# Three moves in the odd layer: where the last projection's first loads land, when attention outputs are transposed, and when the conditioning begins

## The chip, the cores and the metric

The kernel runs on one core of a Trainium2 chip. The metric is device time in microseconds: the median of three runs, 2327.63 us (2325.06 to 2328.44). A separate profiled execution took 2321.26 us, with a span of 2319.5 us between its first and last instruction; all rows of the trace are from that one.

## The reference

One step of a two-layer transformer trunk, for 128 prompt tokens and 512 sample tokens that share weights. Each layer normalizes, applies a shift and a scale that come from a conditioning vector (`silu(cond) @ ada_w + ada_b`, split in shift, scale and gate), projects, runs its mixers, multiplies by SiLU gates, projects out and adds the result times the conditioning gate:

```
hs = rms_norm(xs, norm_g[layer]) * (1.0 + sc_s) + sh_s
cq, ck, cv, cg, dq, dk, dv, dg = split_cols(h @ w_in, ODD_SPLIT)
o1 = attend(cq[:, 0], ck_all[:, 0], cv_all);  o2 = attend(cq[:, 1], ck_all[:, 1], cv_all)
o_c = rms_norm(o1 - lam * o2, c_on) * (1.0 - lam_init)
y_d = merge_heads(attend(q_d, dk_all, dv_all)) * silu(dg)
xs = xs + gt_s * (concat([o_c * silu(cg), y_d]) @ w_out)
```

The second (odd) layer has mixer D, eight heads of grouped-query attention, and mixer C, four heads of differential attention: two softmax maps whose difference weighs the values. The sample tokens attend to 256 cached keys and their own 512.

## The kernel before

All activations lie with features on the partitions and 640 tokens (512 + 128) in the free dimension. A float32 matrix product is made of three matmuls of split operands (`wh*hi`, `wh*lo`, `wl*hi`): ScalarE rounds the high part, VectorE subtracts the low part (`split`, line 241 and 242). A projection's weight column block of 128 is used in four quarters of four row tiles each; a quarter is 24 matmuls of 320 columns, half into `pa`, half into `pb` (lines 276 to 278).

The odd layer's queries and keys are projected by `run_tiles`: 30 jobs of four quarters, 120 quarters in all. After each quarter `slot` advances three kinds of side work: the preparation of the tile that has just been projected (`q_gen`, `k_gen`, `v_gen`), one step (for later jobs 1.1 or 1.5 on average) of a running attention generator, and `rate` steps of `fill1`. `fill1` is `ada_on_dve`: four blocks of the layer's conditioning product that VectorE makes by itself, as 64 multiply-adds into `acc` per block (lines 211 and 213) from weights `adaw` loaded by SyncE (line 207). A block can't begin before the instruction to which it is tied, the weight split that was the latest when the block was emitted (line 202). The tile framework then sets every engine's own order, and pulls instructions that are ready ahead of their place in the program.

`k_gen` transposes the projected keys, scales and rotates them on VectorE (from line 600 to 620, with a power on GpSimd, line 608, between), and TensorE transposes the result back (line 564). `diff_gen` runs one head of mixer C over five query blocks u: `score` (scores into the single PSUM tile `S`, softmax, the difference of the maps, line 1354), `groups` (transposes of the weights, line 732), `weigh` (18 matmuls with the values, lines 1369 to 1371, then the output's norm on VectorE, ScalarE and GpSimd, lines 1373 to 1380) and `out` (two transposes of the normalized `on`, line 1386, and the product with the gate, line 1391). A `yield` ends a step.

The last projection begins with `y1_maker`: for each of 16 row tiles k it loads `yin` from DRAM and splits it into the tile `h` that the matmuls read. The order of the row tiles is 0 to 3, 8 to 11, 12 to 15, 4 to 7. Tiles with k % 8 < 4 land in the buffers `rp` (three) and `stg` (two) (line 1536), which `very_late_gate` also uses for the last two jobs (lines 1486 to 1492); the others, after the pool of the odd layer is closed, in `xr` (line 1122). SyncE's DMA issues go in order: what stands behind a waiting one waits too.

Of the kernel before, what the change touches and what calls it, by code (L numbers as in the profile page):

```python
# [45 lines left out]
SPLIT_AHEAD = 3  # L46
N_FILL0 = 12
FILL0 = 1.2
FILL1 = 1.25
FILL1_FROM = 0  # L50


@with_exitstack
def trunk_kernel(ctx: ExitStack, tc: tile.TileContext, I: dict, O: dict):
# [12 lines left out]
    def psT():  # L67
        return pT.tile([P, 512], F32, tag="T", name="T")
# [226 lines left out]
    def drain(queue):  # L295
        while queue:
            advance(queue, 1)
# [440 lines left out]
    def scores(q, blk, k, segs, masks=()):  # L738
        s = pS.tile([P, 1024], F32, tag="S", name="S")
        bs = slice(blk * P, (blk + 1) * P)  # L740
        for dst, k0, n in segs:
            ms = [(m, o) for m, o in masks if dst <= o < dst + n]
            d, ks = s[:, dst:dst + n], slice(k0, k0 + n)
            PE.matmul(d, q[0][:, bs], k[0][:, ks], start=True, stop=False)  # L744
            PE.matmul(d, q[0][:, bs], k[1][:, ks], start=False, stop=False)
            PE.matmul(d, q[1][:, bs], k[0][:, ks], start=False, stop=not ms)  # L746
            for i, (m, o) in enumerate(ms):
                PE.matmul(s[:, o:o + P], identb, m, start=False, stop=(i == len(ms) - 1))
        return s
# [5 lines left out]
    def blk_plan(blk, banded):  # L755

        if blk == 4:
            return PROMPT_SEGS, (), P, 2 * P, [6]
        if not banded:
            return DENSE_SEGS, (), 128, 896, [0, 1, 2, 3, 4, 5]  # L760
        lo_b, hi_b = max(0, blk - 1), min(3, blk + 1)
        nb = (hi_b - lo_b + 1) * P
        masks = []
        if blk > 0:
            masks.append((mask_lo, 512))
        if blk < 3:
            masks.append((mask_hi, 512 + (blk + 1 - lo_b) * P))
        return ([(256, 0, CTX), (512, CTX + lo_b * P, nb)], masks, 256, 512 + nb,
                [0, 1] + [2 + b for b in range(lo_b, hi_b + 1)])
# [184 lines left out]
    def y_pair(i):  # L954
        t = pools["cur"].tile([P, 2, NT], F32, tag="y", name="y", bufs=3 - st["sets"])
        y[i], y[i + 1] = t[:, 0, :], t[:, 1, :]
        return t
# [376 lines left out]
    def diff_gen(ap, h, v, kq):  # L1334

        gt = gates_back(2 * h)
        t = y_pair(2 * h) if gt is None else gt
        ps, pts, ons, rls = {}, {}, {}, {}

        maps = []  # L1340

        def score(u, m):
            segs, masks, lo, hi, _ = blk_plan(u, False)
            n = hi - lo
            k, q = kq[m]
            s = scores(q, u, k, segs)
            maps.append(soft(ap, 768, s[:, lo:hi], n, q[2][u]))
            if m == 0:
                return
            pp, rr, ll = zip(*maps)  # L1350
            maps.clear()
            w = small.tile([P, 1], F32, tag="w", name="w")
            V.scalar_tensor_tensor(out=w, in0=ll[0], scalar=nlam, in1=rr[1], op0=ALU.mult, op1=ALU.mult)
            V.scalar_tensor_tensor(out=pp[0][:, 0:n], in0=pp[1][:, 0:n], scalar=w, in1=pp[0][:, 0:n],
                                   op0=ALU.mult, op1=ALU.add)
            ps[u], rls[u] = pp[0], rr[0]

        def groups(u):
            n = len(blk_plan(u, False)[4])
            pts[u] = [pt_group(ap, [ps[u][:, i * P:(i + 1) * P] for i in range(c0, min(c0 + 4, n))])  # L1360
                      for c0 in range(0, n, 4)]

        def weigh(u):
            chunks = blk_plan(u, False)[4]
            last = len(chunks) - 1
            o = psT()[:, 0:256]
            for i, c in enumerate(chunks):
                ph, pl = (x[:, (i % 4) * P:(i % 4) * P + P] for x in pts[u][i // 4])
                PE.matmul(o, ph, v[0][:, c, :], start=(i == 0), stop=False)
                PE.matmul(o, ph, v[1][:, c, :], start=False, stop=False)  # L1370
                PE.matmul(o, pl, v[0][:, c, :], start=False, stop=(i == last))
            on = ap.tile([P, 256], F32, tag="on", name="on", bufs=2)
            V.tensor_scalar(on, o, rls[u], None, ALU.mult)
            ssq = small.tile([P, 1], F32, tag="ssq", name="ssq")
            junk = ap.tile([P, 256], F32, tag="junk", name="junk")
            A.activation(junk, on, AF.Square, accum_out=ssq)
            V.tensor_scalar(ssq, ssq, 1.0 / 256, EPS, ALU.mult, ALU.add)
            rn = small.tile([P, 1], F32, tag="rn", name="rn")
            G.tensor_tensor(rn, ssq, half[:, 0:1], op=ALU.pow)
            V.scalar_tensor_tensor(out=on, in0=on, scalar=rn, in1=st["con"], op0=ALU.mult, op1=ALU.mult)  # L1380
            ons[u] = on

        def out(u):
            x = psT()
            for j in range(2):
                PE.transpose(x[:, j * P:(j + 1) * P], ons[u][:, j * P:(j + 1) * P], ident)
            d, x = t[:, :, u * P:(u + 1) * P], x[:, 0:256].rearrange("p (j q) -> p j q", j=2)
            if gt is None:
                A.copy(d, x)
            else:  # L1390
                V.tensor_mul(d, x, d)

        for u in range(7):
            if u >= 2:
                out(u - 2)
            if u < 5:
                score(u, 0)
            if 1 <= u < 6:
                groups(u - 1)
            if u < 6:  # L1400
                yield
            if u < 5:
                score(u, 1)
            if 1 <= u < 6:
                weigh(u - 1)
            if u < 6:
                yield
        save_y(2 * h, 2 * h + 1)
# [64 lines left out]
    def gates_back(i):  # L1473
        if i not in FRONT:
            return None
        t = y_pair(i)
        for j in range(2):
            nc.sync.dma_start(t[:, j, :], gdram[i + j])
        return t
# [36 lines left out]
    for i in (4, 5):  # L1516
        jobs.append((OD["cg"] + i * P, very_late_gate(i)))
    run_tiles(jobs, I["od_w_in"][0], None, fill1, FILL1, fill_from=FILL1_FROM,
              steps=lambda i: brisk.get(i, 1.0))
# [3 lines left out]
    def y1_maker(k):  # L1523
        if k == 12:
            for _ in fill1:
                pass
            drain(attn)
            close("odd")
            open_pool("fin")
            attn.append(forms(ydram))  # L1530
        if k % 8 >= 4:
            late_yin(k)
        else:
            tag, n = (("rp", 3), ("stg", 2))[k % 2]
            t = pools["cur"].tile([P, NT], F32, tag=tag, name="yin", bufs=n)
            nc.sync.dma_start(t, ydram[k])
            split(*new_h(k), t)
# [82 lines left out]
```

## Time and profile before

| | |
|---|---|
| median of three runs | 2327.63 us |
| the profiled execution | 2321.26 us, its span 2319.5 us |
| TensorE busy | 2259.1 us, 97% of the span |
| VectorE busy | 1678.2 us, 72% |
| ScalarE busy | 991.9 us, 43% |
| DMA | 348.18 MB, mean 150 GB/s |
| odd layer's `run_tiles` | begins near 1417 us; the last projection begins near 2075 us |

A busy TensorE is the state to keep, so the rows to read are those in which it stood idle: a row of the timeline gives start, duration, engine, line, operation and, in brackets, the idle time before it and the instruction that ended the idle time. In a row of waits stand the total, the number and the longest. The windows give busy time by engine with the number of instructions, and then the TensorE clock that was granted, as a share of full speed.

### The profile page before, as it was taken

To read this page: it belongs to the slowest core of one execution; us is meant where nothing else is said; L and a number is where in the kernel's file an instruction comes from. 1 tells how busy PE (TensorE), PEld (TensorE's weight loads), DVE (VectorE), ACT (ScalarE), POOL (GpSimd) and SP (SyncE) were. 2 spreads that over 40 slices of the span, in tenths; PEclk is the share of its full clock that TensorE was granted. 3 is DMA by queue.
4 is the path that set the end of the run, shared out by engine and by line. 5 is a ranking of instruction groups with operands and counts; after the bars stand their busy time and mean duration, and the time that the engine had idled before them with its cause. 6 is when DMAs were issued, how large, how long until landed. Compare 5 with 4: busy or idle time off the path is not lost.

```text
span 2319.5 us, 41525 instructions
## 1 busy us (share of the span) xinstructions
PE 2259.1 (97%) x15796; PEld 2182.4 (94%) x15796; DVE 1678.2 (72%) x3364; ACT 991.9 (43%) x2043; POOL 184.0 (8%) x251
## 2 busy tenths in 40 slices
PE   7999999999999999999999999999999999997999
PEld 5699999999999999999999999999999989997999
DVE  4559886786866664988877766778687696576576
ACT  4335432433422222544744445454555454553343
POOL 2110000000000000000100000000001111100001
PEclk9999999999999999999999999999999999999999
DMA  9974545445455543844763335333243333237532
GB/s 354 339 264 124 159 123 159 143 127 163 124 180 155 152 138 120 280 133 138 247 212 113 106 115 168 97 101 97 63 128 106 103 103 92 80 111 244 152 119 70
DMA packets 390056, 348.18 MB, mean 150 GB/s; under 512 B 19362, under 2 KB 327088, under 8 KB 389344
## 3 DMA queue, kind: packets, MB, share of 16 engines
q1 hardware_dynamic: 376960, 296.97, 41.8%
q0 software_dynamic: 12176, 46.39, 5.2%
q8 instruction: 124, 2.03, 0.4%
q10 hardware_dynamic: 720, 2.16, 0.2%
q14 instruction: 76, 0.62, 0.1%
HBM read 304.55 MB, written 40.90 MB: 149 GB/s over the span
## 4 chain that ended last, share of the span: by engine, by line
PE 84%; DVE 6%; DMA 4%; ACT 2%; issue 2%; POOL 1%; SPq 0%; POOLq 0%; ACTq 0%; DVEq 0%
PE pa L276 8%; PE pb L277 8%; PE pa L277 8%; PE pb L276 8%; PE pa L278 8%; PE pb L278 8%; PE pq L535 7%; PE pq L536 7%; PE pq L537 7%; PE T L732 2%; DMA adaw<-in_ada_w 2%; DMA yin<-yd 1%; PE T L178 1%; PE S L744 1%; PE S L746 1%
## 5 line engine op out<-in xcount | busy, mean ns | idle before, releaser
L241 ACT ACTIVATE wh<-raw 128x512 fp32r<-128x512 f32 (+1 forms) x442 | 273.4, 619 | 671.6 <-PE pb L277 565.5
L276 PE MATMUL pa<-h,wh 128*128 128x320 f32 x1520 | 483.8, 319 | 15.8 <-ACT h L241 13.3
L277 PE MATMUL pa<-h,wh 128*128 128x320 f32 x1520 | 474.0, 312 | 1.0 <-DVE h L242 0.6
L278 PE MATMUL pa<-h,wl 128*128 128x320 f32 x1520 | 472.4, 311 | 0.0
L278 PE MATMUL pb<-h,wl 128*128 128x320 f32 x1520 | 471.5, 310 | 0.0
L277 PE MATMUL pb<-h,wh 128*128 128x320 f32 x1520 | 471.0, 310 | 0.0
L276 PE MATMUL pb<-h,wh 128*128 128x320 f32 x1520 | 470.8, 310 | 0.0
L242 DVE TENSOR_TENSOR wl<-raw,wh 128x512 fp32r<-128x512 f32 (+1 forms) x442 | 297.2, 673 | 238.6 <-ACT wh L241 211.9
L213 DVE SCALAR_TENSOR_TENSOR acc<-adaw,sT,acc 128x512 f32<-128x512 f32 (+1 forms) x600 | 359.4, 637 | 12.4 <-DMA adaw<-in_ada_w 11.9
L276 PEld LDWEIGHTS pa<-h,wh 128*128 128x128 f32 x1520 | 286.8, 189 | 29.3 <-ACT h L241 14.9
L277 PEld LDWEIGHTS pa<-h,wh 128*128 128x128 f32 x1520 | 286.9, 189 | 6.0 <-DVE h L242 2.9
L278 PEld LDWEIGHTS pa<-h,wl 128*128 128x128 f32 x1520 | 286.6, 189 | 2.9 <-issue 2.9
L278 PEld LDWEIGHTS pb<-h,wl 128*128 128x128 f32 x1520 | 285.9, 188 | 2.1 <-issue 2.1
L276 PEld LDWEIGHTS pb<-h,wh 128*128 128x128 f32 x1520 | 286.0, 188 | 0.4 <-issue 0.4
L277 PEld LDWEIGHTS pb<-h,wh 128*128 128x128 f32 x1520 | 285.9, 188 | 0.1
L535 PE MATMUL pq<-h,wh 128*128 128x320 f32 x608 | 189.7, 312 | 0.7 <-ACT wh L241 0.7
L536 PE MATMUL pq<-h,wh 128*128 128x320 f32 x608 | 187.9, 309 | 0.0
L537 PE MATMUL pq<-h,wl 128*128 128x320 f32 x608 | 187.8, 309 | 0.0
L718 ACT ACTIVATE p<-S,nm,rq 128x768 f32<-128x768 f32 (+3 forms) x120 | 101.1, 843 | 100.7 <-DVE nm L713 59.5
L535 PE MATMUL pq<-T,wh 128*128 128x320 f32 x456 | 140.9, 309 | 0.0
L537 PE MATMUL pq<-T,wl 128*128 128x320 f32 x456 | 140.9, 309 | 0.0
L536 PE MATMUL pq<-T,wh 128*128 128x320 f32 x456 | 140.9, 309 | 0.0
(337 smaller groups left out, 3890.4 us busy)
## 6 DMA issues: line engine op xcount, KB each, us to landing
adaw<-in_ada_w SPq DMA_DIRECT2D x192, 256.0 KB, 2.9
raw<-in_ev_w_in SPq DMA_DIRECT2D x184, 256.0 KB, 2.9
raw<-in_od_w_in SPq DMA_DIRECT2D x160, 256.0 KB, 2.9
ada<-in_ada_w SPq DMA_DIRECT2D x14, 2048.0 KB, 10.3
adaw<-in_ada_w SPq DMA_DIRECT2D x128, 128.0 KB, 2.1
w<-in_od_w_in SPq DMA_DIRECT2D x24, 512.0 KB, 3.7
yd<-y POOLq DMA_DIRECT2D x32, 320.0 KB, 3.4
yin<-yd SPq DMA_DIRECT2D x32, 320.0 KB, 4.5
```

The lines of the kernel that those rows point to most:

```text
L178: PE.matmul(acc[32 * g:32 * g + 32, 0:wd], sT[:, kt, :], w[:, kt % m, :], start=(i < 4), stop=(i >= KT - 4), tile_position=(0, 32 * g))
L213: V.scalar_tensor_tensor(out=a, in0=w, scalar=sT[:, kt, c:c + 1], in1=a, op0=ALU.mult, op1=ALU.add)
L241: A.activation(hi, x, AF.Copy)
L242: V.tensor_sub(lo, x, hi)
L276: PE.matmul(ps, wh[:, i, :], hi[:, sl], start=(j == js[0] if alone else (pos == 0 and j == 0)), stop=False)
L277: PE.matmul(ps, wh[:, i, :], lo[:, sl], start=False, stop=False)
L278: PE.matmul(ps, wl[:, i, :], hi[:, sl], start=False, stop=(j == js[1] - 1 if alone else (pos == 3 and j == 3)))
L535: PE.matmul(ps, wh[:, j, :], hi, start=(h == 0 and j == 0), stop=False)
L536: PE.matmul(ps, wh[:, j, :], lo, start=False, stop=False)
L537: PE.matmul(ps, wl[:, j, :], hi, start=False, stop=(h == 1 and j == 3))
L718: A.activation(p[:, 0:n], s, AF.Exp, scale=rsc, bias=nm, accum_out=l)
L732: PE.transpose(t[:, i * P:(i + 1) * P], p, ident)
```

## The change

Three edits. `fill1` gets its first step after quarter 8 instead of at once, at 1.3 steps a quarter instead of 1.25. In `diff_gen` the call `out(u - 2)` moves behind the first `yield` of block u, so that it comes one step later, except for the last block's. In `y1_maker` the loads for k = 0 to 3 use the buffers `q0h`, `q0l`, `q1h`, `q1l`, which hold two sets of split queries in turn; the set that comes next is that of the head before the last.

```diff
-FILL1 = 1.25
-FILL1_FROM = 0
+FILL1 = 1.3
+FILL1_FROM = 8
...
         for u in range(7):
-            if u >= 2:
-                out(u - 2)
             if u < 5:
                 score(u, 0)
             if 1 <= u < 6:
                 groups(u - 1)
             if u < 6:
                 yield
+            if u >= 2:
+                out(u - 2)
             if u < 5:
                 score(u, 1)
...
-            tag, n = (("rp", 3), ("stg", 2))[k % 2]
+
+            tag, n = (("q0h", 2), ("q0l", 2), ("q1h", 2), ("q1l", 2))[k] if k < 4 else (("rp", 3), ("stg", 2))[k % 2]
             t = pools["cur"].tile([P, NT], F32, tag=tag, name="yin", bufs=n)
```

VectorE at the start of the odd layer, before. `lp` and `nlam` are the constants of mixer C, `acc` the conditioning sums, `wl` a weight split, `qm` the first query tile's rotation:

```order
L1319 TENSOR_REDUCE ls<-lp 128x2
L211 TENSOR_SCALAR acc_16206<-adaw,sT 128x256
L211 TENSOR_SCALAR acc_16207<-adaw,sT 128x256
L1322 TENSOR_TENSOR nlam<-le 128x1
L213 SCALAR_TENSOR_TENSOR acc_16206<-adaw,sT,acc_16206 128x256
```

The same place now, and the place at which the conditioning now begins, at the second query tile's `qm`:

```order
L1319 TENSOR_REDUCE ls<-lp 128x2
L1322 TENSOR_TENSOR nlam<-le 128x1
L1323 TENSOR_SCALAR nlam<-nlam 128x1
L242 TENSOR_TENSOR wl<-raw,wh 128x512
L242 TENSOR_TENSOR vl<-ctxv,vh 128x256
L242 TENSOR_TENSOR wl<-raw,wh 128x512
L656 TENSOR_TENSOR qm<-qx,tables 128x512
...
L656 TENSOR_TENSOR qm<-qx,tables 128x512
L202 CAST acc_16505<-wl 128x1
L202 CAST acc_16506<-wl 128x1
L211 TENSOR_SCALAR acc_16505<-adaw,sT 128x256
```

Sixty-one conditioning products stood ahead of the first key preparation (line 600) before; now 31 do, and the rest of the block stands behind it.

VectorE at the second key preparation of head 2 of mixer C (`kg` is its first row), before:

```order
L242 TENSOR_TENSOR k0l<-T,k0h 128x256
L242 TENSOR_TENSOR k0l<-T,k0h 128x512
L242 TENSOR_TENSOR k0l<-T,k0h 128x128
L242 TENSOR_TENSOR vl<-vx,vh 128x5x128
L242 TENSOR_TENSOR wl<-raw,wh 128x512 x2
L600 TENSOR_TENSOR kg<-T,gain_rows 128x512
```

The same place now:

```order
L213 SCALAR_TENSOR_TENSOR acc_21895<-adaw,sT,acc_21895 128x256
L213 SCALAR_TENSOR_TENSOR acc_21894<-adaw,sT,acc_21894 128x256
L242 TENSOR_TENSOR wl<-raw,wh 128x512
L213 SCALAR_TENSOR_TENSOR acc_21895<-adaw,sT,acc_21895 128x256
L213 SCALAR_TENSOR_TENSOR acc_21894<-adaw,sT,acc_21894 128x256
L213 SCALAR_TENSOR_TENSOR acc_21895<-adaw,sT,acc_21895 128x256
L213 SCALAR_TENSOR_TENSOR acc_21894<-adaw,sT,acc_21894 128x256
L213 SCALAR_TENSOR_TENSOR acc_21895<-adaw,sT,acc_21895 128x256
L242 TENSOR_TENSOR wl<-raw,wh 128x512
L213 SCALAR_TENSOR_TENSOR acc_21894<-adaw,sT,acc_21894 128x256
L213 SCALAR_TENSOR_TENSOR acc_21895<-adaw,sT,acc_21895 128x256
L213 SCALAR_TENSOR_TENSOR acc_21894<-adaw,sT,acc_21894 128x256
```

The conditioning's last block now lies over both key preparations of head 2 (ahead of the other one eight of its products stand within twelve rows); before, it lay over the second one of head 1.

TensorE at the fourth `out` of head 1 of mixer C, before. `on` is the normalized output, `p` the softmax weights, `h_12900` and the like the activations of a quarter; the block's last `weigh` stands 14 projection matmuls ahead of the `on` row:

```order
L276 MATMUL pa<-h_12900,wh 128x320
L277 MATMUL pa<-h_12900,wh 128x320
L278 MATMUL pa<-h_12900,wl 128x320
L276 MATMUL pb<-h_12882,wh 128x320
L277 MATMUL pb<-h_12882,wh 128x320
L1386 MATMUL T<-ident,on 128x128 x2
L732 MATMUL T<-ident,p 128x128
```

The same `out` now:

```order
L276 MATMUL pb<-h_13150,wh 128x320
L277 MATMUL pb<-h_13150,wh 128x320
L278 MATMUL pb<-h_13150,wl 128x320
L1386 MATMUL T<-ident,on 128x128 x2
L276 MATMUL pb<-h_13159,wh 128x320
L1369 MATMUL T<-vh,pth 128x256
```

It stands behind 39 projection matmuls after the same `weigh`, in the next quarter, and right ahead of the last block's `weigh`.

On SyncE the loads of row tiles 0 to 3 now stand among the weight loads of the last jobs, 13 weight loads earlier than before, and those of tiles 8 to 11 take the places that tiles 0 to 3 had. The loads of row tiles 12 to 15 (line 1122) and everything behind them stand as before.

## The prediction

> **What bounds the kernel now.** I read the page first, for the engine that is nearly always busy, then the windows over the part that the change touches, then TensorE's waits there, and the timeline at the longest of them.
>
> ```profile
> span 2319.5 us, 41525 instructions
> PE 2259.1 (97%) x15796; PEld 2182.4 (94%) x15796; DVE 1678.2 (72%) x3364; ACT 991.9 (43%) x2043; POOL 184.0 (8%) x251
> ...
> 1416.00:1780.00 364.00, 358.55 (x2528) 347.97 (x2527) 275.98 (x630) 184.83 (x397) 30.59 (x30) 1.00 0.37 113
> 1780.00:2097.00 317.00, 303.49 (x2115) 289.96 (x2113) 224.21 (x517) 159.19 (x388) 40.01 (x46) 1.00 0.31 94
> 2097.00:2127.00 30.00, 17.76 (x102) 16.38 (x103) 19.87 (x34) 11.03 (x16) 1.12 (x2) 0.89 0.82 271
> ```
>
> TensorE (first busy figure of a row) is the bound: work taken from another engine is worth nothing unless TensorE waited for it. In the two windows of the odd layer's projections and attentions it stood idle for 364.00 - 358.55 = 5.5 us and 317.00 - 303.49 = 13.5 us, and at the change to the last projection for 12.2 us of 30. That is all that the change can win, beside clock. TensorE's own waits over these windows, with total, number and longest:
>
> ```profile
> PE pa L276 <- ACT h L241: 12.6, 4, 8.4
> PE T L1386 <- DVE on L1380: 7.4, 8, 1.5
> PE T L564 <- DVE m L620: 3.8, 4, 2.1
> PE T L794 <- DVE ptl L242: 1.7, 2, 0.8
> PE S L744 <- ACT p L718: 1.6, 2, 1.1
> ...
> PE T L1386 <- DVE rl L724: 0.5, 1, 0.5
> PE T L564 <- DVE k1l L242: 0.4, 1, 0.4
> ```
>
> Three of these groups answer to the three edits: `h` split from loaded rows to the loads, `on` to the output transposes, `m` (the rotated keys) to the conditioning, which shares VectorE with the key preparation.
>
> ```profile
> 1472.69 0.66 PE L564 MATMUL T<-ident,m 128*128 128x128 f32 x4 [2.08 <-DVE m L620]
> ...
> 1608.68 0.38 PE L794 MATMUL T<-ptl,vh 128*128 128x256 f32 x1 [0.84 <-DVE ptl L242]
> ...
> 1841.82 0.44 PE L1386 MATMUL T<-ident,on 128*128 128x128 f32 x2 [1.45 <-DVE on L1380]
> 1860.92 0.66 PE L564 MATMUL T<-ident,m 128*128 128x128 f32 x4 [1.43 <-DVE m L620]
> 1863.05 0.33 PE L564 MATMUL T<-ident,kg 128*128 128x128 f32 x1 [0.42 <-DVE k1l L242]
> ...
> 1922.23 0.41 PE L1386 MATMUL T<-ident,on 128*128 128x128 f32 x2 [1.23 <-DVE on L1380]
> ...
> 1933.43 0.44 PE L1386 MATMUL T<-ident,on 128*128 128x128 f32 x2 [1.46 <-DVE on L1380]
> 2020.68 0.44 PE L1386 MATMUL T<-ident,on 128*128 128x128 f32 x2 [1.45 <-DVE on L1380]
> 2080.88 0.42 PE L276 MATMUL pa<-h,wh 128*128 128x320 f32 x1 [1.42 <-ACT h L241]
> 2105.17 0.64 PE L276 MATMUL pa<-h,wh 128*128 128x320 f32 x1 [8.37 <-ACT h L241]
> ```
>
> **Part 1: the conditioning eight quarters later.** The same 256 multiply-adds are made; nothing is added or taken away. They come in four bursts, one for each block, 66 instructions and some 27 us each, between which VectorE makes none:
>
> ```profile
> 1420.00:1480.00 60.00, 27.00 (x66) 0.97 0.58 176
> 1480.00:1540.00 60.00, 0.00 (x0) 1.00 0.18 53
> 1540.00:1610.00 70.00, 27.44 (x66) 1.00 0.40 120
> ...
> 1840.00:1920.00 80.00, 27.89 (x66) 1.00 0.43 130
> ```
>
> The first burst holds up the first key preparation:
>
> ```profile
> 1465.11 0.20 ACT L598 ACTIVATION_READ_ACCUMULATOR junk<-T 128x1 f32 x1
> ...
> 1465.34 1.28 DVE L213 SCALAR_TENSOR_TENSOR acc<-adaw,sT,acc 128x256 f32<-128x256 f32 x3 [0.16 <-DMA adaw<-in_ada_w]
> 1466.54 0.68 DVE L600 TENSOR_TENSOR kg<-T,gain_rows 128x512 f32<-128x512 f32 x1
> ...
> 1471.95 0.68 DVE L620 TENSOR_TENSOR m<-m,m 128x512 f32<-128x512 f32 x1
> ```
>
> ScalarE had squared the last transposed block by 1465.3, so VectorE could have scaled the keys before that; it came to them at 1466.54, behind conditioning that waited for its own weights. TensorE, which had nothing else in order, stood for 2.08 us. The price is more than that, because the clock (the third figure from the end of each row) went down behind it:
>
> ```profile
> 1470.00:1474.00 4.00, 1.92 (x15) 1.68 (x14) 3.97 (x9) 1.50 (x3) 0.60 (x1) 1.00 0.20 65
> 1474.00:1477.00 3.00, 3.00 (x14) 2.96 (x13) 0.98 (x2) 0.70 (x2) 0.00 (x0) 0.50 0.55 159
> 1477.00:1480.00 3.00, 3.00 (x21) 3.00 (x21) 0.69 (x1) 0.95 (x2) 0.00 (x0) 0.93 0.00 0
> ...
> 1933.00:1938.00 5.00, 4.57 (x33) 4.50 (x34) 4.66 (x9) 2.11 (x5) 1.11 (x2) 1.00 0.72 237
> ```
>
> Three microseconds at 0.50 lose 1.5, three at 0.93 lose 0.2: 1.7 us, so this wait costs 3.8. (The last row holds the gap of 1.46 us at 1933.43, which left the clock alone.) In the new order 31 of the conditioning's products stand ahead of that key preparation instead of 61. VectorE needs some 0.4 us for each (27.00 / 66), so 30 fewer take 12 us out of its way, while the start comes later by eight quarters; a quarter is 24 matmuls at the pace of these two rows, 0.15 us apart, so 3.6 us, and eight are 29 us:
>
> ```profile
> 1922.73 0.31 PE L276 MATMUL pb<-h,wh 128*128 128x320 f32 x1
> 1922.88 0.31 PE L277 MATMUL pb<-h,wh 128*128 128x320 f32 x1
> ```
>
> From a start near 1446 (the second query's rotation, with no backlog ahead of it), 31 products (12.7 us) and the queries' and weights' own instructions (some 4.6 us) bring VectorE to the keys at 1463 to 1465, where it waits for ScalarE until 1465.3. Then `m` is ready 1.2 to 2 us sooner, and most of the 2.08 goes. I take the whole of it and the clock: -3.8 us. It could be nothing: the last rows ahead of the keys, three products behind a weight split, are the same as before, and if VectorE comes to them as late, the wait stays.
>
> The rest of the first burst now lies over the value rows and the first attention of mixer D. Before, the second burst lay over an attention and cost 0.84 us (the row at 1608.68); I add +0.8, between 0 and twice that. The fourth burst moves by four quarters, off the second key preparation of head 1 (the rows at 1860.92 and 1863.05: 1.43 + 0.42 = 1.85, gone) and onto both of head 2, one with eight products close ahead, the other with ten of the twelve rows shown. Five of ten key preparations stood under a burst and now six do; of those five, two waited (2.08 and 1.85) and three did not (the 3.8 us of the group `m` hold 2.08, 1.43 and 0.3 for two others). So two new ones bring one wait of the smaller size: +1.85, between 0 and two of 3.8. The SyncE queue carries as many `adaw` loads, only later, and weight loads run up to five quarters (18 us) ahead of use: nothing there.
>
> [...] The measurement decides, and every wait of 2 us is priced with 1.7 of clock.
>
> **Part 2: outputs a step later.** The two transposes and the product with the gate are the same. Of the 7.4 + 0.5 us that TensorE stood before `on`, the last blocks' (the rows with 1.45, 1.46 and 1.45, each the fifth of its head) are not moved: 4.4 us stay. The other 3.5 us are six waits of blocks 0 to 3, the longest 1.23. There the transposes stood 14 projection matmuls (2.1 us) behind the weighing that makes `on`, and now stand behind 39 (5.9 us); the lag from weighing to `on` was 2.1 + 1.23 = 3.3 us, so the wait is covered with 2.5 us to spare. Behind the later transposes on TensorE stands the next `weigh`, which has other work before it; in PSUM the output's tile now takes the place that the first group of transposed weights leaves, and that has long been copied. I take -3.0 us, between -3.5 and 0 (a VectorE that is full would delay `on` too).
>
> **Part 3: the loads.** Four `yin` loads go 13 weight loads earlier on SyncE, behind head 2's last scores, which read those buffers and stand in quarters 106 and 107 of TensorE's order. The next weight loads behind them are for quarter 113 and on, so a wait there has six quarters (21 us) of cover. The 1.42 us at 2080.88 was row tile 2, whose buffer the last gate held:
>
> ```profile
> 2074.69 0.82 DVE L1491 TENSOR_TENSOR gg<-yg,gg 128x640 f32<-128x640 f32 x1
> ...
> 2080.09 0.74 ACT L241 ACTIVATE h<-yin 128x640 fp32r<-128x640 f32 x1 [1.50 <-DMA yin<-yd]
> 2080.73 0.44 ACT L718 ACTIVATE p<-S,nm,rq 128x128 f32<-128x128 f32 x1
> ```
>
> That wait goes. But tiles 10 and 11 now wait for the same gate, and ScalarE's order has their splits ahead of the last block's softmax `p`. `S` is a single tile, so the other map's scores wait for `p`. TensorE would be there at about 2080.3, and `p` ends at about 2081.2 if the load lands as late as before: 0.9 us or more of the 1.42 come back. I take -0.4, between -1.4 and +0.6. The 8.37 us at 2105.17, for row tiles 12 to 15, stay: their loads stand behind the same four weight loads and the last output, and the whole end only moves earlier with TensorE.
>
> **Sum.** -3.8 + 0.8 - 1.85 + 1.85 - 3.0 - 0.4 = -6.4 us. The profiled execution took 2321.26 us (1.8 outside its span), so the new one would take 2314.9; it lay 6.4 below the median of the runs shown, 2327.63, and from that median the forecast is 2321.2, 0.27% less. A measurement of this kernel can tell about 0.2%, 4.7 us, from no change.
>
> **Rivals.** (a) The waits only change places. The first keys wait as before (their last rows are the same), a key preparation of head 2 takes over from that of head 1, the loads' wait comes back in full at `S`: only the 3.0 of the outputs are left, less the 0.8 at the first attention: 2325.4, no change that can be told. For it: VectorE was full in every burst, and the bursts are as long as before. Against: 30 products fewer ahead of the first keys. (b) Slower: the last burst holds up both key preparations of head 2, each by 2.08 and 1.7 of clock as at 1472.69, and the first keeps its own. +7.6 - 1.85 + 0.8 and, with VectorE full over heads 1 and 2, half of the outputs' gain, -1.5: +5.1, 2332.7. It decides as soon as VectorE comes to the scaling of both by 2 us too late. For it: ten products right ahead of the second. Against: three of five preparations under a burst came in time. (c) The clock went down at 1474 for another reason than the gap ahead of it, and will do so again; then the first keys win 2.1, not 3.8, and the time is 2322.9, hardly faster. For it: the gap of 1.46 us left the clock alone; against: 0.50 directly behind the gap. [...] (d) The edits don't do what they say: the order shows that they do, so this has no chance of its own.
>
> **How the numbers follow.** The forecast has 0.50, (a) 0.30, (b) 0.15, (c) 0.05. Faster by over 0.2%: the forecast and, by a hair, (c), less what the spread of the terms takes from the forecast: 0.52. Same: (a) and that part: 0.33. Slower: 0.15. The range: the low end takes the waits of head 2 as not there (-1.85) and the parts' best ends, -0.5 for the outputs, -1.0 for the loads, -0.8 for the first attention: 2317.1, and 2 us for the scatter of the runs shown: 2315. The high end takes in (a) and most of the way to (b): 2331.
>
> **What would show it.** Right: no TensorE wait of over 0.5 us at the first key transposes, with a clock of 1.00 behind it; waits on `on` only for last blocks, some 4.4 us together; a wait of about a microsecond at `S` or `h` near 2075; the 8 us before row tiles 12 to 15 as before. Wrong: a wait of 2 us or more at a key transposition of head 2 with 0.50 behind it (b), or the total idle time of the two odd windows unchanged (a).

## The result, and the profile after

The changed kernel took 2316.21 us, median of five runs (2312.96 to 2316.9), against 2327.63 for the kernel before; the ratio is 0.9949 with a 95% interval of 0.9935 to 0.9964. That is 11.4 us less where 6.4 were forecast. The profiled execution took 2312.96 us, its span 2311.2.

First, from the page, each engine's busy time: the same instructions, and 3.4 us less of it on TensorE.

```profile
PE 2255.7 (98%) x15796; PEld 2181.3 (94%) x15796; DVE 1677.4 (73%) x3364; ACT 991.5 (43%) x2043; POOL 182.2 (8%) x251
```

Then the windows over the same stretches of the program as before, their later edges set eight microseconds earlier:

```profile
1416.00:1780.00 364.00, 358.67 (x2537) 347.59 (x2537) 269.01 (x607) 185.12 (x398) 29.93 (x32) 1.00 0.37 111
1780.00:2089.00 309.00, 301.79 (x2119) 290.43 (x2117) 231.32 (x542) 159.88 (x389) 39.74 (x46) 1.00 0.33 101
2089.00:2119.00 30.00, 18.61 (x108) 17.23 (x109) 20.87 (x36) 11.53 (x17) 1.12 (x2) 0.89 0.84 281
```

TensorE's idle time in them went from 5.5 to 5.3, from 13.5 to 7.2 and from 12.2 to 11.4 us. So the gain lies in the second window, over the heads of mixer C, and beside it in the clock. TensorE's waits by group:

```profile
PE pa L276 <- ACT h L241: 10.1, 3, 8.2
PE S L744 <- ACT p L718: 2.6, 3, 1.2
PE T L1386 <- DVE on L1380: 2.6, 2, 1.4
PE T L564 <- DVE m L620: 2.3, 5, 0.8
...
PE T L1386 <- DVE mod L155: 0.5, 1, 0.5
PE T L1386 <- DVE ptl L242: 0.4, 1, 0.4
...
PE T L1386 <- DVE kg L600: 0.4, 2, 0.2
```

The output transposes (line 1386) stood for 7.9 us in all and now stand for 2.6 + 0.5 + 0.4 + 0.4 = 3.9. The single waits, from the timeline:

```profile
1473.30 0.66 PE L564 MATMUL T<-ident,m 128*128 128x128 f32 x4 [0.81 <-DVE m L620]
1475.29 0.33 PE L564 MATMUL T<-ident,kg 128*128 128x128 f32 x1 [0.32 <-DVE k0l L242]
...
1627.54 0.45 PE L744 MATMUL S<-k1h,q1h 128*128 128x384 f32 x1 [1.22 <-ACT p L718]
...
1771.34 0.66 PE L564 MATMUL T<-ident,m 128*128 128x128 f32 x4 [0.65 <-DVE m L620]
1773.60 0.33 PE L564 MATMUL T<-ident,kg 128*128 128x128 f32 x1 [0.55 <-DVE k1l L242]
...
1841.69 0.41 PE L1386 MATMUL T<-ident,on 128*128 128x128 f32 x2 [1.19 <-DVE on L1380]
1858.46 0.66 PE L564 MATMUL T<-ident,m 128*128 128x128 f32 x4 [0.17 <-DVE m L620]
...
1929.22 0.41 PE L1386 MATMUL T<-ident,on 128*128 128x128 f32 x2 [1.38 <-DVE on L1380]
1945.41 0.65 PE L564 MATMUL T<-ident,m 128*128 128x128 f32 x4 [0.47 <-DVE m L620]
...
2074.97 0.39 PE L744 MATMUL S<-k1h,q1h 128*128 128x256 f32 x1 [0.57 <-ACT p L718]
2097.18 0.64 PE L276 MATMUL pa<-h,wh 128*128 128x320 f32 x1 [8.18 <-ACT h L241]
```

The 2.08 us at the first key transposes are 0.81 and 0.32; head 1's second key preparation (1858.46) waits for 0.17 instead of 1.85; that of head 2 (1945.41) waits for 0.47; the 8 us before row tiles 12 to 15 are there as before. Head 2's second key preparation had waited for 0.16 us in the kernel before:

```profile
1950.26 0.66 PE L564 MATMUL T<-ident,m 128*128 128x128 f32 x4 [0.16 <-DVE m L620]
```

To compare profiles by the part that the edits touch, the time from the odd layer's first query norm (line 661) to the last matmul before row tile 12 is used from here on: in the kernel before 2105.17 - 8.37 - 1432.68 = 664.1 us, in the changed one 2097.18 - 8.18 - 1434.55 = 654.5, so 9.7 less. The first of these two rows stands at 1431.8 to 1438.3 in the profiles of this study, whatever the kernel, so what lies ahead of the odd layer scatters by 6.5 us, and whole spans of single executions compare badly.

### The profile page after: what moved, and what is told of

Its sections match the earlier page's. It is cut to its first block, busy times and chain, and to the rows that moved or that the text cites. A ratio compares the mean times of both kernels' runs of the same rounds, so it can differ in the third digit from the quotient of the medians.

```text
span 2311.2 us, 41533 instructions
## 1 busy us (share of the span) xinstructions
PE 2255.7 (98%) x15796; PEld 2181.3 (94%) x15796; DVE 1677.4 (73%) x3364; ACT 991.5 (43%) x2043; POOL 182.2 (8%) x251
## 3 DMA queue, kind: packets, MB, share of 16 engines
q10 hardware_dynamic: 720, 2.16, 0.3%
## 4 chain that ended last, share of the span: by engine, by line
PE 49%; DVE 4%; DMA 2%; ACT 1%; issue 1%; POOL 1%; SPq 0%; POOLq 0%; DVEq 0%; ACTq 0%
PE pq L535 7%; PE pq L537 7%; PE pq L536 7%; PE pb L277 3%; PE pb L276 3%; PE pa L278 3%; PE pa L276 3%; PE pb L278 3%; PE pa L277 3%; PE T L732 1%; DMA adaw<-in_ada_w 1%; PE S L744 1%; PE T L564 1%; PE S L746 1%; PE S L745 1%
```

## The experiments

The theory (A): each edit takes away TensorE's waits in its own group, and the three add up. The rivals: (B) the edits work only together, because each draws the order anew; (C) the clock went down behind the first keys for another reason than the gap there. Each ratio is to runs of the kernel before on the same chip; "stretch" is the time just described, from one profile each.

| kernel | median, us | ratio to the kernel before (95%) | stretch, us |
|---|---|---|---|
| before, two profiles | 2325.35 (first set of runs) | 1 | 664.1, 667.1 |
| conditioning alone | 2321.63 | 0.9980 (0.9971 to 0.9989) | 663.1 |
| outputs alone | 2320.92 | 0.9980 (0.9972 to 0.9989) | 660.0 |
| loads alone | 2324.69 | 0.9997 (0.9988 to 1.0006) | 664.9 |
| all three again | 2316.46 | 0.9963 (0.9950 to 0.9975) | 654.4 |
| outputs and loads | 2319.22 | 0.9972 (0.9959 to 0.9984) | 659.9 |
| conditioning and outputs | 2316.91 | 0.9964 (0.9952 to 0.9977) | 654.9 |
| conditioning and loads | 2320.97 | 0.9977 (0.9967 to 0.9987) | 660.3 |
| before, weight loads left out | 2321.95 | 0.9981 (0.9971 to 0.9990) | 659.2 |
| changed, weight loads left out | 2315.14 | 0.9955 (0.9942 to 0.9967) | 654.2 |
| changed, pool closed later | 2306.61 | 0.9921 (0.9909 to 0.9934) | |
| the same, row sums later | 2308.49 | 0.9921 (0.9907 to 0.9936) | |

**The conditioning alone.** The kernel before with

```diff
-FILL1 = 1.25
-FILL1_FROM = 0
+FILL1 = 1.3
+FILL1_FROM = 8
```

> The kernel before with the conditioning's edit alone (first step after quarter 8, 1.3 steps a quarter). Theory A, each edit removes the TensorE waits of its own group and the three add up: the first key transposes wait about 1.1 us instead of 2.08 and the clock behind them stays at 1.00 (-1.0 and -1.7), head 1's second key preparation no longer waits (-1.8), the second one of head 0 now waits about 1.2; in all -3 to -4 us, with the waits on `on` left at about 7.9 us and the 1.42 us at `h` left. Rival B, the edits work only together (the order is drawn anew by each, and the waits change places): less than 1 us, or a wait of 1 us or more at a key preparation of head 2 that the changed kernel did not have. Rival C, the clock went down at 1474 for another reason than the gap ahead of it: the gap at the first key transposes is short and the clock is nevertheless near 0.50 behind it, -2 us or less in all.

```profile
1472.96 0.66 PE L564 MATMUL T<-ident,m 128*128 128x128 f32 x4 [0.95 <-DVE m L620]
...
1920.84 0.43 PE L1386 MATMUL T<-ident,on 128*128 128x128 f32 x2 [2.45 <-DVE on L1380]
...
1950.86 0.66 PE L564 MATMUL T<-ident,m 128*128 128x128 f32 x4 [1.44 <-DVE m L620]
```

2321.63 us, 3.7 less than the kernel before: the size that A gave. The first keys do what was forecast, and so does head 1's second key preparation (0.17 us). But 2.45 us at `on` and 1.44 us at head 2's second key preparation (the wait that the prediction had priced at 1.85) stand in this profile and not in that of all three edits. The second of them is the sign that B had named. VectorE's rows ahead of them point at a cause, a conditioning product that waited for its weights:

```profile
1916.70 0.88 DVE L213 SCALAR_TENSOR_TENSOR acc<-adaw,sT,acc 128x256 f32<-128x256 f32 x2 [1.92 <-DMA adaw<-in_ada_w]
...
1942.05 1.67 DVE L213 SCALAR_TENSOR_TENSOR acc<-adaw,sT,acc 128x256 f32<-128x256 f32 x4 [1.89 <-DMA adaw<-in_ada_w]
```

**The outputs alone.** The kernel before with `out(u - 2)` behind the first `yield`, as in the change.

> The kernel before with the later output transposes alone. Theory A: the waits on `on` fall from 7.9 to about 4 us, only the last blocks' being left; the first key transposes wait 2.08 us as before, with a clock of 0.50 behind them; -4 us, down to -5 with the waits on `p` that go as well. Rival B: the waits on `on` become waits at the score tile or at the weights' transposes one step on, and the time falls by less than 1.5 us. Rival C (clock): the same long gap at the first keys, and the clock behind it at 1.00 this time.

```profile
PE T L564 <- DVE m L620: 5.3, 4, 3.4
PE T L1386 <- DVE on L1380: 3.9, 3, 1.5
```

2320.92 us, 4.4 less, and the waits on `on` are 3.9 us: A. The first keys waited for 3.4 us in this execution, with 0.50 behind.

**The loads alone.** The kernel before with the buffers of `y1_maker` as in the change.

> The kernel before with the four loads in the queries' buffers alone. Theory A: the 1.42 us at `h` near 2081 goes, 0.6 us come at `S`, and the end of the odd layer is otherwise the same: -0.9 us, not to be told from no change, with 8.4 us left in front of row tiles 12 to 15. Rival B: the loads wait behind head 2's last scores and hold up weight loads behind them on SyncE: +1 us or more, with a wait on weights near quarter 113. Clock: 2.08 us at the first key transposes and 0.50 behind them, as before; 1.00 there would say that the gap alone does not set it.

```profile
1475.81 0.44 PE L564 MATMUL T<-ident,m 128*128 128x128 f32 x2 [2.32 <-DVE m L620]
...
2085.72 0.39 PE L744 MATMUL S<-k1h,q1h 128*128 128x256 f32 x1 [0.95 <-ACT p L718]
```

2324.69 us, 0.7 less, not to be told from nothing: the wait at `h` is gone and 0.95 us stand at `S`, as A has it. The clock answered otherwise: 2.32 us at the first keys and no lower clock behind. That spoke for C and called for a closer look (the windows are shown further on).

**All three, on the same chip.**

> The changed kernel itself once more, beside the three parts on the same chip: 11 us under the kernel before (2316), by which the sum of the three parts is judged. Theory A: the three parts' gains come to within 3 us of this one's. Rival B: they come to less than half of it, or to more than it by 4 us. Its profile should show the waits of the first profile again: 8.2 us before row tiles 12 to 15, about 3.9 us on `on`, 0.81 us at the first key transposes with a clock of 1.00 behind, and, if what its first profile lost near 920 to 980 us was chance, about 2 us less there.

2316.46 us, 8.9 less than before; the parts alone came to 3.7 + 4.4 + 0.7 = 8.8. The stretch again took 654.4 us.

**One edit left out at a time.** These are the changed kernel with the old lines of `FILL1` and `FILL1_FROM`, with the old `tag, n` line, and (run last) with `out` back at its old place.

> The changed kernel without the conditioning's edit (outputs later and loads in the queries' buffers). Theory A, the three edits add up (alone they took 3.7, 4.4 and 0.7 us off, 8.8 together, and all three at once 8.9): 5.1 us under the kernel before, so 3.7 us above the changed kernel, with the first key transposes waiting 2 us or more and, where that wait brings the clock down, 1.65 us more; waits on `on` about 4 us. Rival B, interaction: the conditioning's edit alone showed a new wait of 2.45 us on `on` with a clock of 0.50 behind it and 1.44 us at head 2's second key preparation, which the changed kernel does not have; if the later outputs take these away, the edit is worth more beside them than alone, and this kernel lies 5 to 7 us above the changed one.

> The changed kernel without the loads' edit (conditioning and outputs later). Theory A (additive): 8.1 us under the kernel before, 0.7 above the changed kernel, not to be told from it; the wait of some 1 us at `h` near 2076 is back and that at `S` gone. Rival B (the loads' edit works only beside the other two, or holds up the last outputs): 3 us or more away from the changed kernel on either side. In both: no wait over 1.5 us on `on`, and 0.9 us at the first key transposes with a clock of 1.00.

> The changed kernel without the outputs' edit (conditioning later and loads in the queries' buffers). Theory A (additive, by the edits alone): 4.4 us under the kernel before, 4.5 above the changed kernel. Theory F, the outputs' edit also removes the clock's losses: in the kernels that have it TensorE keeps a clock of 1.00 from the second query block of head 1 to row tile 12, while those without it (the kernel before profiled twice, and two of the parts) lost one stretch of 3.4 us at half clock, 1.7 us, near 1921 to 1933 in three of four profiles, behind a wait of 2.3 to 2.5 us on `on`. Then it is 5 to 8 us above the changed kernel, and its profile shows 8 us or more of waits on `on`; if one of them is over 2 us and leaves TensorE busy for less than half of a stretch of 3.4 us, 0.50 stands behind it.

By medians, against the kernel before of their own runs: 2325.1 - 2319.22 = 5.9 without the conditioning, 2325.1 - 2316.91 = 8.2 without the loads, 2327.47 - 2320.97 = 6.5 without the outputs. Beside the 8.9 of all three, the conditioning is worth 3.0, the loads 0.7 and the outputs 2.4; by the ratios 2.1, 0.2 and 3.3. That fits A within the intervals, which are about 3 us to either side here. The stretches would have the conditioning worth more beside the others (659.9 - 654.4 = 5.5) than alone (1.0 or 4.0, by the profile of before that is taken); single profiles don't settle that. Theory F, which wanted 5 us or more for the outputs beside the rest, is not borne out by the medians. The wait on `on` was there in the last kernel (2.00 us), and it left the clock alone, although TensorE was busy for only 1.49 us of that piece of 3.41 us (from 1916.64 on), less than the half that F had set.

**The kernel before, profiled again.**

> The kernel before, unchanged, profiled a second time: it tells what in its first profile was chance. Its first profiled execution took 2321.26 us, under all 27 timed ones of the same kernel (2322.64 to 2329.75). Theory: the waits in the odd layer are the same within 0.3 us each (2.1 us at the first key transposes, 1.85 at head 1's second key preparation, about 8 on `on`, 8.4 before row tiles 12 to 15), and the 4 us by which it was quick are clock that went down at fewer of the gaps of 2 us or more, or shorter waits for loads near 920 to 980. Rival: the waits on `on` themselves differ by 2 us or more from execution to execution, and one trace cannot carry a term of that size.

```profile
1478.42 0.66 PE L564 MATMUL T<-ident,m 128*128 128x128 f32 x4 [2.58 <-DVE m L620]
...
1928.96 0.41 PE L1386 MATMUL T<-ident,on 128*128 128x128 f32 x2 [2.28 <-DVE on L1380]
```

This execution took 2332.61 us, longer than every timed run of the kernel before (up to 2331.86). The first half of the theory fails: the first keys waited for 2.58 us instead of 2.08, head 1's second key preparation for 2.16 instead of 1.85. Its other half, the clock, is borne out in part: from the odd layer's start to the last projection two pieces of some 3.4 us stand at 0.50, against one in the first profile. The rival's 2 us are not reached, with 9.1 us at the output transposes against 7.9, but it has a point: the same wait on `on` was 1.23 us in the first profile and 2.28 here, 1.05 more. The order is the same. VectorE's row ahead of it, first in the earlier profile, then in this one:

```profile
1918.45 0.88 DVE L213 SCALAR_TENSOR_TENSOR acc<-adaw,sT,acc 128x256 f32<-128x256 f32 x2 [0.55 <-DMA adaw<-in_ada_w]
```

```profile
1925.18 0.88 DVE L213 SCALAR_TENSOR_TENSOR acc<-adaw,sT,acc 128x256 f32<-128x256 f32 x2 [1.60 <-DMA adaw<-in_ada_w]
```

VectorE waited 1.60 - 0.55 = 1.05 us longer for the load, and that is the whole difference. The windows behind it, TensorE's busy time first and the clock third from the end:

```profile
1926.40:1929.82 3.42, 1.14 (x9) 0.91 (x9) 1.70 (x5) 0.76 (x3) 0.55 (x1) 1.00 0.00 0
1929.82:1933.23 3.41, 3.41 (x16) 3.37 (x15) 0.99 (x3) 1.15 (x5) 0.00 (x0) 0.50 0.00 0
```

The clock was at 0.50 for 3.41 us, another 1.7 lost. So in this order a late weight load goes through VectorE to TensorE. That made a new theory, D: loads, not products, are what the conditioning costs.

**Without the weight loads.** Both kernels, with two loads in each block and the rest of its products made from those two tiles, so that the sums come out as other numbers:

```diff
-                w = ap.tile([P, wd], F32, tag=wt[i % 3], name="adaw", bufs=bufs)
+                w = ap.tile([P, wd], F32, tag=wt[i % 3], name="adaw", bufs=bufs) if parts == 1 or i < 2 else w
...
-                nc.sync.dma_start(w, I["ada_w"][l, kt * P:(kt + 1) * P, c0:c0 + wd])
+                (parts == 1 or i < 2) and nc.sync.dma_start(w, I["ada_w"][l, kt * P:(kt + 1) * P, c0:c0 + wd])
```

> The kernel before, in which the conditioning that VectorE makes beside the odd layer loads only two of each block's 64 weight tiles and multiplies those over and over: 248 of 256 loads are left out, so the shift, scale and gate of those blocks are other numbers; the 512 multiply-adds are all made. Theory D, the loads: VectorE takes its instructions in order, and what made the rows behind late was a product that stood waiting for its `adaw` load (0.2 to 1.9 us each in the traces, different from execution to execution), so without the loads the wait at the first key transposes falls from 2.1 to 2.6 us to under 1.2, head 1's second key preparation from 1.8 to under 0.5, the wait on `on` near 1925 from 1.2 to 2.5 us to under 0.8, the clock stays at 1.00 in all three places, and the time is 4 to 8 us under the kernel before. Rival E, the products themselves: VectorE's 27 us of work a burst fill it, the waits stay within 0.4 us, and the time is within 2 us.

> The changed kernel with the same loads left out (again 248 of 256, all products made). Theory D: what the change's conditioning edit and part of the outputs' edit won was shelter from late loads, so without loads the change is worth less: this kernel is 3 to 6 us under the same kernel without the change, not 9 to 11, and 0 to 3 us under the changed kernel. Rival E (the products): it is as far under the kernel without loads as the changed kernel is under the kernel before, 9 to 11 us.

A block has 32 loads and 64 products, so 120 of 128 loads are left out and 256 products made; the texts above count both double. In the kernel without the change there is no idle row at the first key transposes at all, the clock stays at 1.00 from the odd layer's start to the last projection, and of the two waits that are left one is smaller and one is not. VectorE's row at the first keys comes first:

```profile
1470.56 0.69 DVE L600 TENSOR_TENSOR kg<-T,gain_rows 128x512 f32<-128x512 f32 x1 [0.62 <-ACT junk L598]
...
1862.78 0.66 PE L564 MATMUL T<-ident,m 128*128 128x128 f32 x4 [1.42 <-DVE m L620]
...
1923.33 0.41 PE L1386 MATMUL T<-ident,on 128*128 128x128 f32 x2 [0.74 <-DVE on L1380]
```

At the first keys VectorE now waits for ScalarE, although 64 products stand ahead of it instead of 61. So D holds for the first keys and for `on`, and E (the products themselves) for head 1's second key preparation. In time the loads cost the kernel before 2.7 us by medians (4.4 by the ratio, 4.9 to 7.9 in the stretch), where D had said 4 to 8, and the changed one 1.3 by medians (0.2 in the stretch).

What the change is worth without loads, these two runs don't tell. They differ by 2321.95 - 2315.14 = 6.8 us, between D's 3 to 6 and E's 9 to 11, and 2 us less than the 8.9 with loads, which is within the intervals. Moreover, leaving out the loads drew VectorE's order anew: in the second kernel, too, all 64 products of the first block now stand ahead of the first key preparation. Its first product starts at 1431.0, 5.8 us ahead of the first query norm, as in the kernel before (5.9); in the changed kernel it started at 1448.1, 13.6 us behind it. So at the first block this kernel lacks the conditioning's later start. That part of the change's gain is shelter from late loads is therefore not shown in time, and the effect of the loads' own traffic was not tested apart. (In the second kernel `S` waited for 2.59 us near 2075 with half a clock behind, so its stretch could be shorter.)

**A step further.** What is left is the wait of 8.2 us before row tiles 12 to 15. SyncE's own rows in the changed kernel show why: their loads (line 1122) stand behind four weight loads that wait for their buffers, for 19.4 us in all, 11.6 of it in two waits that ended with a split `wl` of VectorE.

```profile
2078.08 12.37 SPq L254 DMA_DIRECT2D raw<-in_od_w_out  x4
2090.55 1.49 SPq L1122 DMA_DIRECT2D yin<-yd  x3
```

This kernel closes the odd layer's pool at row tile 4, the last four in order, so that 12 to 15 load into the odd layer's buffers:

```diff
-        if k == 12:
+        if k == 4:
...
-        if k % 8 >= 4:
+        if 4 <= k < 8:
```

> A step beyond the changed kernel: the pool of the odd layer is closed at row tile 4, the last in order, instead of at row tile 12, so that row tiles 12 to 15 land in `rp` and `stg` and only 4 to 7 in `xr`. Theory A: the 8.2 us before row tiles 12 to 15 come from their loads standing behind the pool's end (the last output and the copies that follow); with the loads ahead of it most of the wait goes, 5 us or more, and the clock behind it stays up (1.7 us more); of that 1.5 us return at row tiles 4 to 7, whose loads now are the late ones but have 8 row tiles of matmuls as cover: 5 to 7 us under the changed kernel. Rival B: the loads are late for their buffers' sake (`rp` and `stg` are read by the last gate and by row tiles 8 to 11) or for the DMA's, which moves 370 GB/s there: the wait only moves to row tiles 4 to 7, and the time is within 2 us of the changed kernel's or above it.

```profile
2068.01 8.22 SPq L1537 DMA_DIRECT2D yin<-yd  x6
...
2098.00 0.41 PE L276 MATMUL pa<-h,wh 128*128 128x320 f32 x1 [1.67 <-ACT h L241]
2108.57 0.69 PE L564 MATMUL T<-ident,xr 128*128 128x128 f32 x2 [3.00 <-DVE xr L1117]
```

2306.61 us, 18.5 less than before (ratio 0.9921, 0.9909 to 0.9934) and 9.9 under the changed kernel's 2316.46 (in another set of runs), more than the 5 to 7 expected. In the row of six, the last four loads are those of row tiles 12 to 15; they are issued from 2070.9 on instead of 2090.6, the 8.2 us are gone, and 1.67 + 3.00 us come in their place. Waits at the end of the profile account for some 6 to 7 us of the 9.9; the rest was not traced. The loads moved ahead of the weight loads and got other buffers at once, so which of the two had held them is not told apart. This is faster than both kernels. The last kernel tried to win the 3.00 as well, by one empty step ahead of the row sums:

```diff
-            attn.append(forms(ydram))
+            attn.append(f for g in ((0,), forms(ydram)) for f in g)
```

> The kernel with the odd layer's pool closed at row tile 4, and the row sums for the last-but-one step (`sx`, `T`) begun one quarter later. In that kernel TensorE stood 3.0 us behind `xr` (line 1117) near 2108 with the clock at 0.50 for some 6 us behind; the residual sum stood on VectorE behind five instructions of these sums and a weight split (0.48 + 0.49 + 0.48 + 0.68 + 0.48 = 2.6 us) that now come after it. Theory: the wait falls to about the 1.3 us that it has in the changed kernel, and a gap that short leaves the clock alone: 1.7 to 3.5 us less than that kernel, 20 to 22 under the kernel before. Rival: the sums are missed later, at the matmuls that read `T`, or the load of `xr` sets the 3.0 us: within 1 us of it.

```profile
2102.43 0.41 PE L276 MATMUL pa<-h,wh 128*128 128x320 f32 x1 [1.93 <-ACT h L241]
2112.32 0.44 PE L564 MATMUL T<-ident,xr 128*128 128x128 f32 x2 [0.79 <-DVE xr L1117]
2132.94 0.44 PE L564 MATMUL T<-ident,xr 128*128 128x128 f32 x2 [1.48 <-DVE xr L1117]
```

The wait fell to 0.79, but another of 1.48 came at the next sum, and the clock went down behind that one and behind the 1.93. 2308.49 us, 16.1 less than before and not the 20 to 22 expected; the ratio is the same 0.9921 as that of the kernel without the empty step.

## Why the prediction was right, and where its sizes were off

The direction and the mechanism held in the main: waits on VectorE went, nothing new of their size came, the end only moved. The forecast took 6.4 us off; the two sets of runs gave 11.4 and 8.9. One of its signs failed: it allowed 0.5 us at the first key transposes, and 0.81 stood there. By its own steps:

- **First keys, -3.8.** 2.08 us became 0.81 + 0.32, and the clock stayed up: -0.95 - 1.7 = -2.7. The step "I take the whole of it" was 1.1 too much. Its reason, 30 fewer products ahead of the keys, was not the whole one either: without the weight loads no wait stood there although 64 products were ahead.
- **First attention under the burst, +0.8.** No idle row stands between 1475.29 and the 0.83 us near 1608 that was there before. But 1.22 us came at `S` at 1627.54, and the kernels with the conditioning's edit and its weight loads all have that (1.05 to 1.27); the one without the loads doesn't.
- **Head 1's second key preparation, -1.85.** 1.85 became 0.17: -1.7.
- **Head 2's, +1.85.** This step failed: the first of them has no wait in either kernel, and the second one's 0.16 became 0.47, so +0.3. Of the seven profiles with the conditioning's edit and its loads, only that of the conditioning alone had more than 1 us here (1.44, with a wait of 1.89 for a load ahead of it); in the kernel with conditioning and loads, whose outputs are not moved either, it was 0.48. Another 1.2 us that the step did not have came at head 0's second key preparation (1771.34 and 1773.60). The count "five under a burst, two waited" was a poor guide: without the weight loads the wait at the first keys was gone and that at head 1's second key preparation stayed, so the two had different causes.
- **Outputs, -3.0.** 7.9 became 3.9 us: -4.0 in the first pair of profiles, -5.2 against the second profile of before (8.6 + 0.5). The last blocks' waits fell from 1.45, 1.46, 1.45 to 1.19, 1.38 and 0.48, so "are not moved" was true of the order and not of the wait. Moreover the first profile had been lucky: its 1.23 us at 1922 were 2.28, 2.45 and 2.35 in three other executions of this order of outputs with the weight loads, each with 0.50 behind, 1.7 us that the sum did not have (and 2.00, with no loss of clock, in a fourth).
- **Loads, -0.4.** 1.42 us went and 0.57 came at `S`: -0.85; alone, the edit gave 0.7. The mechanism is the one foreseen, and 0.57 was a lucky draw: 1.13 us stood at `S` in the second profile of the changed kernel.
- **The end.** 8.37 and 8.18 us, as forecast.

These steps add to -2.7 + 1.2 - 1.1 (`S` at 1702.71 before, 1.14 us, gone) - 1.7 + 0.3 + 1.2 - 4.0 - 0.85, and small changes at `S` near 1805 (+0.4), at the weights' transposes (-0.5) and at line 225 (+0.5): -7.3 of the 9.7 in the stretch. The other 2.4 us stand in no group of waits. Most of them lie in TensorE's busy time: over the stretch it fell from 645.36 to 641.90 us for the same 4527 matmuls, 3.5 less, of which the clock at the first keys is 1.7; why the other 1.8 went is open. That the time fell into the range is in part luck: the two larger misses, head 2's and the outputs', both made the gain larger than forecast, and the range ended 1.2 us below the result.

Rival (a) fell with the second window, where TensorE's idle time went from 13.5 to 7.2 us; rival (b) with 0.47 us and no wait at head 2's two key preparations.

**The clock.** Rival (c), C above, failed as a forecast, since the clock stayed at 1.00 behind the first keys, but its doubt was justified. The sum priced "every wait of 2 us" with 1.7 of clock. The price is right where it falls due, the condition is not. All fourteen traces were cut in pieces of 3.41 us, beginning where the clock went down. First the kernel before at its first keys:

```profile
1470.57:1473.99 3.42, 1.33 (x11) 1.30 (x11) 3.40 (x8) 1.21 (x3) 0.60 (x1) 1.00 0.24 75
1473.99:1477.40 3.41, 3.41 (x15) 3.37 (x14) 0.98 (x2) 0.70 (x2) 0.00 (x0) 0.50 0.49 141
```

Then the kernel with outputs and loads, in which a gap of 2.95 us at the first keys was cut in two by an edge at 1475.78 and a gap of 1.99 us at head 1 was not:

```profile
1477.43 0.66 PE L564 MATMUL T<-ident,m 128*128 128x128 f32 x4 [2.95 <-DVE m L620]
1864.05 0.66 PE L564 MATMUL T<-ident,m 128*128 128x128 f32 x4 [1.99 <-DVE m L620]
```

Its windows on the grid:

```profile
1472.37:1475.78 3.41, 2.12 (x15) 1.87 (x14) 2.35 (x6) 0.90 (x2) 1.65 (x2) 1.00 0.04 13
1475.78:1479.19 3.41, 1.75 (x13) 1.75 (x14) 3.36 (x8) 0.60 (x1) 0.22 (x1) 1.00 0.41 125
1479.19:1482.60 3.41, 3.41 (x26) 3.41 (x25) 0.87 (x3) 1.65 (x4) 0.00 (x0) 1.00 0.32 92
1861.49:1864.90 3.41, 1.42 (x12) 1.18 (x11) 3.41 (x9) 1.06 (x3) 0.53 (x1) 1.00 0.13 43
1864.90:1868.31 3.41, 3.41 (x14) 3.36 (x14) 2.94 (x7) 0.71 (x2) 0.00 (x0) 0.50 0.80 240
```

The longer gap cost no clock and the shorter one did. From 1417 us on, in these fourteen profiles, the clock went with TensorE's busy time within one piece of a fixed grid: of the pieces that ran at 1.00, those with up to 1.42 us busy were all followed by one at 0.50 (22 of them), those with 1.75 and over by one at 1.00, and of eight between (1.49 to 1.66) two were followed by 0.50 and six by 1.00. Busy time is not the whole measure: at the change of layers, near 1124 us, pieces of 2.05 us (outputs and loads) and 2.39 us busy (the changed kernel's second profile), filled mostly with transposes and with matmuls of a single column, were followed by 0.50. The grid did not move with the work: the two falls of the kernel before, at 1473.99 and 2102.04, are 628.05 us apart, 184 pieces of 3.413, and those of the changed kernel at 974.40 and 2093.97 are 1119.57 us apart, 328 pieces of 3.413.

Whether transposes counted for less than other matmuls in this is not shown. One comparison speaks against it: the piece below, of the kernel with the loads alone, was busy for 1.60 us, of which matmuls other than transposes cover only some 0.97, and has 1.00 behind it, while a piece of 1.66 us without any transpose (2100.69, the last kernel) had 0.50 behind it. One pair is little, and the pieces near 1124 us can't decide it, since they hold single-column matmuls as well.

```profile
1859.75:1863.16 3.41, 1.60 (x13) 1.35 (x12) 3.41 (x8) 0.90 (x2) 0.60 (x1) 1.00 0.07 26
1863.16:1866.58 3.42, 3.02 (x21) 2.69 (x20) 3.29 (x8) 0.88 (x2) 0.00 (x0) 1.00 0.80 234
```

From the odd layer's start up to the last projection, the profiles without the conditioning's edit but with the weight loads (before twice, outputs, loads, outputs and loads) lost one or two such pieces each, six in five profiles; those with it lost one in seven (the conditioning alone). That is 1.2 against 0.14 a profile; at 1.7 us each, an estimate of the clock's part in the gain is 1.8 us. What a wait cost went with where an edge of the grid fell: at the first keys one stood just ahead of the wait in the first profile of the kernel before (1470.57, the wait from 1470.61 on) and inside it in that of outputs and loads (1475.78, the wait from 1474.48 on). Which of the two an execution gets is taken here for chance; that was not tested.

What stays open: whether the edits help each other, as the stretches suggest, or not, as the medians say; how much of the gain is shelter from late loads; and why the weight loads land 1 us later in one execution than in another.

## What to carry to other kernels

Work that filled VectorE's spare time cost by its loads here, 2.7 us by the medians without them, and not by its instructions alone: a product that waited 1.60 us for its load (the kernel before, profiled again), or 1.92 (the conditioning alone), held up the output's norm behind it in VectorE's order, and TensorE waited for that for 2.28 and 2.45 us. So such a filler should not stand ahead of rows on which the bottleneck waits, and a consumer is best placed so late that such a lateness is covered. A wait of 2 us seen in one trace is one draw (that at the first keys was 2.08 and 2.58 us in two executions of the kernel before): look at what it hung on, and profile the kernel a second time before a term of the sum rests on it. And when a stretch of loads stands in a queue behind transfers that wait for buffers, move the loads ahead of them first: here that, with other buffers for them, was worth 9.9 us, as much as the three edits together.

## What the runs showed of the hardware that was not expected

- TensorE's clock fell to 0.50 in pieces of 3.41 us on a fixed grid (falls 184 and 328 pieces apart in the two kernels' first profiles), which is 1.7 us lost in each. From 1417 us on, in fourteen profiles, it fell behind every piece in which TensorE was busy for up to 1.42 of the 3.41 us, and behind none with 1.75 or more. So a gap of 2.95 us, cut in two by an edge of the grid, passed without a loss, and gaps of 1.99 us (1.42 busy) and even 1.48 us (with shorter ones around it, 1.62 busy) did not.
- The weight load at one and the same place in VectorE's order held VectorE up for 0.55 us in one execution and for 1.60 in another.
